# Softmax normalisation one step later in VectorE's queue: an MLA and stick-breaking trunk

## The chip, the cores and the metric

The kernel runs on one core of one Trainium2 chip. The metric is the device time of one execution in microseconds (us). Before the change it is 683.92 us, the median of three runs (682.63 to 685.81 us). The engines are named as the profile names them: PE (TensorE's matmuls), PEld (TensorE's weight loads), DVE (VectorE), ACT (ScalarE), POOL (GpSimd) and SP (the queue that issues the DMAs).

## The reference

The input is 512 positions of width 1024 in float32. A first layer is multi-head latent attention (MLA, 16 heads), a second one is stick-breaking attention that reads a shared K/V; each has a SiLU gate, an output projection and a gated per-layer embedding. The change touches the softmax of the first layer alone:

```
logits = jnp.einsum('bhqd,bhkd->bhqk', qi, k, preferred_element_type=jnp.float32) * scale
mask = s_idx[None, :] <= t_idx[:, None]
w = jax.nn.softmax(jnp.where(mask, logits, -jnp.inf), axis=-1)
return jnp.einsum('bhqk,bhkd->bhqd', w.astype(v.dtype), v)
```

Queries go in blocks of 128, so block j sees (j + 1) x 128 keys.

## The kernel before, in words

Every float32 product is made of three matmuls of high and low parts (`mm3`, L132 to L136). The MLA stage is a software pipeline of 64 steps, 16 heads by 4 query blocks (`layer`, L810). One step of the front (`mla_front`, L598) is:

- three score matmuls on PE into a PSUM tile of tag `s`, of which there are two (L604);
- the masking pass on DVE (L609; the lists of order below call it ISA): scores times the query's scale plus the mask into `e`, and the row's minimum into `sm`;
- Exp on ACT in place, with the row sum into another column of `sm` (L611);
- the reciprocal of that sum on DVE (L612);
- the product of `e` with it, on POOL (L614) or, for blocks 0 and 1 of the first eight heads, on DVE (L617).

Four steps later `pt_evac` (L555) transposes the normalised `e` on PE (L565, recorded at L130), and ACT and DVE split the result into high and low parts `pt` (L570, L571). After the fourth block of a head, `av` (L573) multiplies by V; ACT and DVE add its two halves (L591, L592: the head sum). `prep` of the next heads transposes q and k (`head_t`, L540) and splits them into `qk` (L548, L549, L551, L552). Between the steps stand matmuls of other work (the `windows` of L899: projections of the next four heads, gates, first halves of the output projection). Their PSUM tiles have tag `g`, two of them in this stage; what frees one is its evacuation, for a half projection the residual addition at L781, for a gate the product at L440, followed by a Sigmoid on ACT (L447) and a product on POOL (L448).

The tile framework orders each engine's instructions by a simulated timeline and by priorities: front, transposes and AV products have an offset of 50 (L46). Between the masking pass and the reciprocal of one step nothing but the data dependency decides.

Of the kernel before, what the change touches and what calls it, by code (L numbers as in the profile page):

```python
# [16 lines left out]
P = 128  # L17
S = 512
# [60 lines left out]
class Trunk:  # L79
    def __init__(self, ctx, tc, A):  # L80
        self.tc, self.nc, self.A = tc, tc.nc, A
        self.cp = ctx.enter_context(tc.tile_pool(name="cp", bufs=1))
        self.sp = ctx.enter_context(tc.tile_pool(name="sp", bufs=1))
        self.pp = ctx.enter_context(tc.tile_pool(name="pp", bufs=1, space=PSUM))
        self.dp = ctx.enter_context(tc.tile_pool(name="dp", bufs=1, space=DRAM))
        self.n = 0
        self.lin = False
        self.last_pe = None
        self.later = None

    BUFS = {"A": 8, "B": 10, "qk": 8, "hat": 6, "gate": 8, "v": 2, "f": 6, "e": 8, "ws": 3, "wh": 3, "wl": 3, "R": 1,
            "sm": 16, "smg": 3, "g": 2, "s": 2, "t": 4}
# [505 lines left out]
    def mla_front(self, h, j, qh, ql, kh, kl, sm, V):  # L598
        nc, v = self.nc, self.nc.vector
        n = (j + 1) * P  # L600
        nn = max(n, 2 * P)
        js = slice(j * P, n)
        ps = self.ps([P, S], "s")
        self.mm3(ps[:, 0:nn], qh[:, js], ql[:, js], kh[:, 0:nn], kl[:, 0:nn], True, True)  # L604
        e = self.t([P, S], F32, "e")
        st = self.t([P, 4], F32, "sm")
        i = j * GH + h % GH

        v.tensor_tensor_reduce(out=e[:, 0:n], in0=ps[:, 0:n], in1=self.mask[:, S - n:S], scale=sm[:, 1, i:i + 1],  # L609
                               scalar=3.0e38, op0=ALU.add, op1=ALU.min, accum_out=st[:, 0:1])  # L610
        nc.scalar.activation(e[:, 0:n], e[:, 0:n], AF.Exp, bias=st[:, 0:1], scale=-1.0, accum_out=st[:, 2:3])  # L611
        v.reciprocal(out=st[:, 3:4], in_=st[:, 2:3])  # L612
        if j >= (2 if h < NH // 2 else 0):
            nc.gpsimd.tensor_scalar(out=e[:, 0:n], in0=e[:, 0:n], scalar1=st[:, 3:4], scalar2=1.0,  # L614
                                    op0=ALU.mult, op1=ALU.mult)
        else:
            v.tensor_scalar(out=e[:, 0:n], in0=e[:, 0:n], scalar1=st[:, 3:4], scalar2=None, op0=ALU.mult)  # L617
        return e

    def sb_group(self, g, res):  # L620
        nc, A, v = self.nc, self.A, self.nc.vector
# [188 lines left out]
    def layer(self, windows, prep, front, pair, prep_lead, lead, av_lag, off):  # L810
        hp = self.tc.high_priority
        heads, es = {}, {}
        NS = NH * NT
        GS = GH * NT
        done = [0] * NG
        for i in range(-prep_lead, NS + lead + av_lag):
            ip = i + prep_lead
            if ip < NS:
                g = ip // GS
                if ip % NT == 0:  # L820
                    with hp(offset=off[0]):
                        heads[ip // NT] = prep(ip // NT, *self.groups[g])
                n, gen = windows[g]
                while done[g] * GS < n * (ip % GS + 1):
                    next(gen, None)
                    done[g] += 1
                if ip % GS == GS - 1:
                    for _ in gen:
                        pass
            if 0 <= i < NS:  # L830
                with hp(offset=off[1]):
                    es[i] = front(i // NT, i % NT, *heads[i // NT])
            b = i - lead
            if 0 <= b < NS:
                h, j = divmod(b, NT)
                if j > 0:
                    with hp(offset=off[2]):
                        self.pt_evac(h, j - 1, es.pop(b), es.pop(b - 1) if j == 1 else None)
            c = b - av_lag
            if 0 <= c < NS and c % NT == NT - 1:  # L840
                h = c // NT
                with hp(offset=off[3]):
                    self.av(h, heads[h][-1])
                if h % 2:
                    pair(h // 2)
# [203 lines left out]
```

## Time and profile before

| | |
|---|---|
| median of three runs | 683.92 us |
| the profiled execution | 683.51 us, span 681.7 us |
| busy: PE, PEld, DVE, ACT, POOL | 666.2, 560.9, 476.7, 400.7, 356.8 us |
| chain that ended last, by engine | PE 89%, ACT 4%, DVE 4%, POOL 1% |
| MLA stage | about 85 to 262 us of the span |

Matmuls are pipelined and their ends are modelled: one of 512 columns is listed with about 0.4 us but the next starts 0.227 us after it. An engine's idle time is listed before the instruction that ended it, with the instruction that released it. Engines take their own instructions in order, so a waiting instruction holds those behind it.

### The profile page before, as it was taken

The page shows a single profiled execution, that of the slowest core. Times are in us where ns is not written, and L with a number is a line of the kernel's source. Part 1 is how long each engine was busy: PE and PEld are TensorE (multiplying, and loading weights), DVE is VectorE, ACT ScalarE, POOL GpSimd, SP SyncE. Part 2 cuts the span into 40 slices and gives each one's busy share as a digit, 9 for nine tenths or more (in the row PEclk, how much of TensorE's full clock was granted, in tenths as well). Part 3 has the DMA queues.
Part 4 walks back from the last instruction along what each step waited for, and adds up shares of the span by engine and source line. Part 5 has one row for each costly group of instructions (what it writes and reads, how often), then busy time and mean ns, then how long its engine had stood idle before and what let it go on. Part 6 is the DMA issues. An engine that isn't in the chain of part 4 may idle for free.

```text
span 681.7 us, 10052 instructions
## 1 busy us (share of the span) xinstructions
PE 666.2 (98%) x3598; PEld 560.9 (82%) x3598; DVE 476.7 (70%) x868; ACT 400.7 (59%) x812; POOL 356.8 (52%) x293
## 2 busy tenths in 40 slices
PE   8989999999998999999999999999999999999997
PEld 6778898989877888888789788779879877788886
DVE  6866489987986774846853886876886889654332
ACT  7266496987988664444533666566665777432221
POOL 5737678776795550035443663775856677100130
PEclk9989999999999999999989999999999999999999
DMA  7331302100133110734332222111221222442321
GB/s 242 116 120 56 109 32 66 62 17 17 35 110 105 62 62 32 210 118 136 119 128 62 94 87 67 59 68 34 91 67 59 64 93 84 162 125 93 107 80 62
DMA packets 21762, 59.82 MB, mean 88 GB/s; under 512 B 2896, under 2 KB 3664, under 8 KB 21712
## 3 DMA queue, kind: packets, MB, share of 16 engines
q1 hardware_dynamic: 21712, 59.18, 26.9%
q8 instruction: 28, 0.46, 0.3%
q14 instruction: 22, 0.18, 0.1%
HBM read 54.97 MB, written 4.19 MB: 87 GB/s over the span
## 4 chain that ended last, share of the span: by engine, by line
PE 89%; ACT 4%; DVE 4%; issue 1%; POOL 1%; DMA 0%; ACTq 0%; POOLq 0%
PE g L127 41%; PE t L127 25%; PE s L127 16%; PE t L130 6%; DVE A L161 1%; ACT L447 1%; ACT wh L143 1%; DVE e L609 1%; DVE ptl L571 0%; DMA e<-in_xT 0%; POOL f L326 0%; DVE f L804 0%; ACT L611 0%; ACT f L447 0%; ACT e L611 0%
## 5 line engine op out<-in xcount | busy, mean ns | idle before, releaser
L127 PE MATMUL g<-A,wh 128*128 128x512 f32 x560 | 182.6, 405 | 2.1 <-ACT f L802 1.4
L143 ACT CAST wh<-ws 128x1024 fp32r<-128x1024 f32 (+2 forms) x92 | 90.2, 982 | 106.3 <-issue 41.0
L144 DVE TENSOR_TENSOR wl<-ws,wh 128x1024 fp32r<-128x1024 f32 (+2 forms) x72 | 96.8, 1346 | 47.0 <-ACT wh L143 45.9
L127 PEld LDWEIGHTS g<-A,wh 128*128 128x128 f32 x560 | 99.6, 189 | 25.4 <-issue 3.2
L127 PE MATMUL g<-A,wl 128*128 128x512 f32 x280 | 110.9, 396 | 0.7 <-POOL wl L344 0.7
L182 POOL TENSOR_TENSOR ws<-ws,gc 128x1024 f32<-128x1024 f32 x24 | 52.2, 2177 | 62.7 <-DMA ws<-in_w_sq 25.2
L698 POOL TENSOR_TENSOR e<-e,e 128x384 f32<-128x384 f32 (+1 forms) x48 | 61.9, 1309 | 20.0 <-DVE e L697 17.1
L570 ACT CAST pth<-t 128x384 fp32r<-128x384 f32 (+1 forms) x96 | 49.6, 518 | 32.0 <-PE t L130 31.3
L571 DVE TENSOR_TENSOR ptl<-t,pth 128x384 fp32r<-128x384 f32 (+1 forms) x96 | 56.5, 593 | 14.8 <-ACT pth L570 14.3
L127 PEld LDWEIGHTS g<-A,wl 128*128 128x128 f32 x280 | 52.9, 189 | 13.2 <-POOL wl L344 1.6
L127 PE MATMUL t<-A,wh 128*128 128x512 f32 (+1 forms) x192 | 59.1, 393 | 0.0
L130 PE MATMUL t<-ident,e 128*128 128x128 f32 x320 | 55.4, 272 | 0.0
L697 DVE TENSOR_TENSOR_SCAN e<-e,maskb 128x384 f32<-128x384 f32 (+1 forms) x32 | 45.8, 1471 | 8.2 <-ACT e L686 8.2
L130 PEld LDWEIGHTS t<-ident,e 128*128 128x128 f32 x320 | 40.4, 140 | 7.3 <-POOL e L614 0.2
L144 POOL TENSOR_TENSOR wl<-ws,wh 128x1024 fp32r<-128x1024 f32 (+2 forms) x20 | 40.0, 2002 | 12.2 <-ACT wh L143 10.7
L127 PE MATMUL s<-qk,qk 96*128 96x256 f32 (+1 forms) x192 | 44.4, 338 | 1.4 <-ACT qk L548 0.7
L614 POOL TENSOR_SCALAR e<-e,sm 128x384 f32<-128x384 f32 (+3 forms) x48 | 27.6, 579 | 33.3 <-DVE sm L612 28.7
L611 ACT ACTIVATE e<-e,sm 128x128 f32<-128x128 f32 (+1 forms) x64 | 36.3, 568 | 12.6 <-DVE sm L609 10.8
L127 PE MATMUL g<-wh,B 128*128 128x384 f32 (+1 forms) x136 | 43.4, 376 | 0.3 <-DVE v L538 0.3
L127 PE MATMUL g<-wh,A 128*128 128x256 f32 x208 | 42.4, 289 | 0.0
L127 PEld LDWEIGHTS t<-A,wh 128*128 128x128 f32 (+1 forms) x192 | 35.1, 184 | 8.3
L127 PE MATMUL t<-ptl,v 128*128 128x256 f32 (+2 forms) x128 | 39.5, 329 | 1.8 <-DVE ptl L571 1.8
(291 smaller groups left out, 1607.2 us busy)
## 6 DMA issues: line engine op xcount, KB each, us to landing
ws<-in_w_pg SPq DMA_DIRECT2D x16, 512.0 KB, 3.6
ws<-in_w_g SPq DMA_DIRECT2D x8, 512.0 KB, 3.2
ws<-in_w_o SPq DMA_DIRECT2D x16, 256.0 KB, 2.6
ws<-in_w_k SPq DMA_DIRECT2D x8, 512.0 KB, 3.6
ws<-in_w_sq SPq DMA_DIRECT2D x8, 512.0 KB, 3.5
ws<-in_w_v SPq DMA_DIRECT2D x8, 512.0 KB, 3.6
ws<-in_w_sg SPq DMA_DIRECT2D x8, 512.0 KB, 3.5
ws<-in_w_o SPq DMA_DIRECT2D x8, 512.0 KB, 3.6
```

The lines of the kernel that those rows point to most:

```text
L127: return self.pe(self.nc.tensor.matmul(*a, **kw))
L130: return self.pe(self.nc.tensor.transpose(*a))
L143: nc.scalar.copy(out=wh, in_=src)
L144: lo_engine.tensor_tensor(out=wl, in0=src, in1=f32(wh), op=ALU.subtract)
L161: (lo_engine or nc.vector).tensor_tensor(out=lo, in0=src, in1=f32(hi), op=ALU.subtract)
L182: nc.gpsimd.tensor_tensor(out=ws, in0=ws, in1=gain.unsqueeze(2).to_broadcast((P, nk, P)), op=ALU.mult)
L570: nc.scalar.copy(out=views[0], in_=ps)
L571: nc.vector.tensor_tensor(out=views[1], in0=ps, in1=f32(views[0]), op=ALU.subtract)
L611: nc.scalar.activation(e[:, 0:n], e[:, 0:n], AF.Exp, bias=st[:, 0:1], scale=-1.0, accum_out=st[:, 2:3])
L614: nc.gpsimd.tensor_scalar(out=e[:, 0:n], in0=e[:, 0:n], scalar1=st[:, 3:4], scalar2=1.0, op0=ALU.mult, op1=ALU.mult)
L697: v.tensor_tensor_scan(out=x, data0=x, data1=mask[:, ::-1], initial=0.0, op0=ALU.mult, op1=ALU.max)
L698: nc.gpsimd.tensor_tensor(out=b[:, 0:n], in0=b[:, 0:n], in1=om[:, 1:n + 1], op=ALU.mult)
```

## The change

The reciprocal and the product of a step are put off to the next step's front. There, right after the masking pass of the new step has been issued, the old step's reciprocal is issued with an ordering edge behind that pass on DVE; then its product. The last step's pair is issued without an edge, one turn later. The arithmetic and the number of instructions in the source stay the same.

```diff
-        v.tensor_tensor_reduce(out=e[:, 0:n], in0=ps[:, 0:n], in1=self.mask[:, S - n:S], scale=sm[:, 1, i:i + 1],
+        low = v.tensor_tensor_reduce(out=e[:, 0:n], in0=ps[:, 0:n], in1=self.mask[:, S - n:S], scale=sm[:, 1, i:i + 1],
                                scalar=3.0e38, op0=ALU.add, op1=ALU.min, accum_out=st[:, 0:1])
         nc.scalar.activation(e[:, 0:n], e[:, 0:n], AF.Exp, bias=st[:, 0:1], scale=-1.0, accum_out=st[:, 2:3])
-        v.reciprocal(out=st[:, 3:4], in_=st[:, 2:3])
+        self.norm_step(low)
+        self.unnormed = lambda: self.mla_norm(h, j, e, st)
+        return e
+
+    def norm_step(self, behind=None):
+
+        if self.unnormed is not None:
+            r = self.unnormed()
+            if behind is not None:
+                self.tc.add_manual_dep(r.ins, behind.ins.name,
+                                       mybir.DependencyInfo(mybir.DependencyClass.NoSync, mybir.DependencyReason.DATA),
+                                       reason="order")
+        self.unnormed = None
+
+    def mla_norm(self, h, j, e, st):
+        nc, v = self.nc, self.nc.vector
+        n = (j + 1) * P
+        r = v.reciprocal(out=st[:, 3:4], in_=st[:, 2:3])
         if j >= (2 if h < NH // 2 else 0):
...
-        return e
+        return r
...
             if 0 <= i < NS:
                 with hp(offset=off[1]):
                     es[i] = front(i // NT, i % NT, *heads[i // NT])
+            if i == NS:
+                self.norm_step()
```

Lines move by 1 up to the masking pass (L609 becomes L610, L611 becomes L612), the reciprocal becomes L630, POOL's product L632, and L781 becomes L799. Since the framework orders all engines anew, rows move on PE, DVE, ACT and POOL through the whole MLA stage; SP's list stays as it was. In the rows below a tile's number tells it apart; with the change the same tile mostly has a number lower by 2.

**First place: ACT around steps 44 to 46, where gates' Sigmoids stand among Exps.** The rows L447 (then L448) are Sigmoids, L611 (then L612) Exps; the 128x128 and 128x256 Exps are steps 44 and 45. Before:

```order
## ACT: 750 rows
L447 ACT_TABLE_LOAD
L447 ACTIVATE f_2287<-gate_1771 128x512
L548 CAST qk_2327<-t_2322 96x512
L570 CAST pth_110<-t_2387 128x384
L143 CAST wh_2366<-ws_2364 128x512
L447 ACTIVATE f_2290<-gate_2192 128x512
L570 CAST pth_110<-t_2425 128x3x128
L160 CAST A_1339<-f_1214 128x512
L160 CAST A_1629<-f_1482 128x512
L570 CAST pth_110<-t_2441 128x4x128
L551 ACTIVATE qk_2453<-t_2448,hs 96x512
```

With the change, from the second Exp load of the piece on:

```order
## ACT: 752 rows
L612 ACT_TABLE_LOAD
L612 ACTIVATE e_2497,sm_2498<-e_2497,sm_2498 128x128
L161 CAST A_1337<-f_1212 128x512
L612 ACTIVATE e_2516,sm_2517<-e_2516,sm_2517 128x256
L161 CAST A_1627<-f_1480 128x512
L448 ACT_TABLE_LOAD
L448 ACTIVATE f_2288<-gate_2190 128x512
L161 CAST A_1903<-f_1763 128x512
L161 CAST A_2246<-f_2086 128x512
L612 ACT_TABLE_LOAD
L612 ACTIVATE e_2563,sm_2564<-e_2563,sm_2564 128x384
```

Before, the Sigmoids of gates 5 and 6 (gate_1771, gate_2192) stood under one load; now that of gate 6 (gate_2190) has moved down between the Exps of steps 45 and 46, with a load of its own and another one for the Exp behind it.

**Second place: DVE at steps 46 and 47, around the residual addition L781 (then L799), whose tile is gate_2362 (then gate_2360).** Before:

```order
L440 TENSOR_TENSOR gate_2282<-g_2210,R_678 128x512
L609 ISA e_2565,sm_2566<-s_2561,mask,smg_1281 128x384
L609 ISA sm_2566 128x1
L609 ISA e_2598,sm_2599<-s_2594,mask,smg_1281 128x512
L609 ISA sm_2599 128x1
L592 TENSOR_TENSOR f_2402<-t_2393,f_2402 64x512
L612 RECIPROCAL sm_2566<-sm_2566 128x1
L612 RECIPROCAL sm_2599<-sm_2599 128x1
L781 TENSOR_TENSOR gate_2362<-g_2337,f_2360 128x512
```

With the change:

```order
L610 ISA e_2596,sm_2597<-s_2592,mask,smg_1279 128x512
L610 ISA sm_2597 128x1
L630 RECIPROCAL sm_2564<-sm_2564 128x1
L441 TENSOR_TENSOR gate_2280<-g_2208,R_678 128x512
L550 TENSOR_TENSOR qk_2461<-t_2455,qk_2460 96x512
L593 TENSOR_TENSOR f_2400<-t_2391,f_2400 64x512
L572 TENSOR_TENSOR ptl_108<-t_2522,pth_106 128x384
L593 TENSOR_TENSOR f_2400<-t_2528,f_2400 64x512
L799 TENSOR_TENSOR gate_2360<-g_2335,f_2358 128x512
L162 TENSOR_TENSOR A_2540<-f_2400,A_2540 128x512
L610 ISA e_2644,sm_2645<-s_2640,mask,smg_1830 128x128
L630 RECIPROCAL sm_2597<-sm_2597 128x1
```

The reciprocal of step 47 (sm_2597) has moved behind the masking pass of step 48 and so behind the residual addition; the gate product, a qk split, a pt split and a head sum now stand ahead of that addition.

**Third place: PE ahead of the first score matmuls of step 44 (tile s_2495, then s_2493).** Before:

```order
L127 MATMUL t_2393<-ptl_108,v_1493 128x256
L127 MATMUL g_2210<-A_126,wh_2206 128x512 x2
L130 MATMUL t_2425<-ident,e_2264 128x128 x3
L127 MATMUL g_2210<-A_126,wl_2207 128x512
L127 MATMUL g_2210<-A_158,wh_2206 128x512
L127 MATMUL s_2495<-qk_2327,qk_2318 128x256
L127 MATMUL s_2514<-qk_2327,qk_2318 128x256
```

With the change:

```order
L128 MATMUL t_2391<-ptl_108,v_1491 128x256
L131 MATMUL t_2423<-ident,e_2262 128x128 x2
L131 MATMUL t_2439<-ident,e_2298 128x128 x2
L131 MATMUL t_2423<-ident,e_2262 128x128
L131 MATMUL t_2439<-ident,e_2298 128x128 x2
L128 MATMUL s_2493<-qk_2325,qk_2316 128x256
L128 MATMUL s_2512<-qk_2325,qk_2316 128x256
L128 MATMUL g_2114<-A_331,wh_2110 128x512 x2
```

Four matmuls of the second gate (g_2210) and the last three of the first (two of them the last row here, the third some rows further) have moved behind these scores, and four transposes of step 39 (t_2439) ahead of them.

## Rows read from the trace of the kernel before

**Rows 1.** The page, busy time, share of the span and instructions:

```profile
PE 666.2 (98%) x3598; PEld 560.9 (82%) x3598; DVE 476.7 (70%) x868; ACT 400.7 (59%) x812; POOL 356.8 (52%) x293
```

**Rows 2.** Stretches: length, busy time (instructions) by engine, clock, DMA share, GB/s:

```profile
core 0: us, PE busy (x) PEld busy (x) DVE busy (x) ACT busy (x) POOL busy (x), PEclk, DMA share, GB/s
...
185.00:210.00 25.00, 22.22 (x116) 17.88 (x115) 18.14 (x39) 22.57 (x38) 22.78 (x20) 1.00 0.32 96
210.00:240.00 30.00, 30.00 (x180) 26.35 (x179) 22.39 (x57) 20.23 (x49) 13.85 (x17) 1.00 0.27 89
...
sum 187.00, PE 183.19 PEld 159.88 DVE 146.03 ACT 145.74 POOL 124.58; mean PE 20.35 PEld 17.76 DVE 16.23 ACT 16.19 POOL 13.84
```

**Rows 3.** Waits of PE, 75 to 262 us: total us, times, longest:

```profile
PE g L127 <- DVE gate L781: 2.1, 1, 2.1
PE s L127 <- ACT qk L548: 0.7, 1, 0.7
PE s L127 <- ACT v L537: 0.4, 1, 0.4
PE s L127 <- DVE sm L609: 0.4, 2, 0.2
PE g L127 <- DVE v L538: 0.3, 1, 0.3
```

**Rows 4.** Waits of all engines, 75 to 262 us:

```profile
POOL e L614 <- DVE sm L612: 28.7, 17, 3.5
...
DVE sm L612 <- ACT e L611: 10.2, 15, 1.4
...
PEld t L130 <- POOL e L614: 0.2, 1, 0.2
```

**Rows 5.** DVE in order of time: start, length, instruction, idle before:

```profile
208.06 0.16 DVE L612 RECIPROCAL sm<-sm 128x1 f32<-128x1 f32 x1 [1.34 <-ACT e L611]
208.76 0.17 DVE L612 RECIPROCAL sm<-sm 128x1 f32<-128x1 f32 x1 [0.54 <-ACT e L611]
208.84 0.69 DVE L781 TENSOR_TENSOR gate<-g,f 128x512 f32<-128x512 f32 x1
```

**Rows 6.** PE in order of time:

```profile
193.00 0.51 PE L127 MATMUL s<-qk,qk 96*128 96x256 f32 x2 [0.69 <-ACT qk L548]
...
209.59 0.73 PE L127 MATMUL g<-B,wh 128*128 128x512 f32 x2 [2.09 <-DVE gate L781]
```

**Rows 7.** Groups by shape, 75 to 262 us: busy us, mean ns, idle before:

```profile
L612 DVE RECIPROCAL sm<-sm 128x1 f32<-128x1 f32 x64 | 9.8, 155 | 10.4 <-ACT e L611 10.2
...
L611 ACT ACT_TABLE_LOAD x4 | 5.1, 1283 | 0.1
...
L447 ACT ACT_TABLE_LOAD x3 | 3.8, 1283 | 0.7 <-DVE gate L440 0.7
```

**Rows 8.** DVE in order of time, steps 26 and 27:

```profile
147.52 0.16 DVE L612 RECIPROCAL sm<-sm 128x1 f32<-128x1 f32 x1 [0.38 <-ACT e L611]
147.81 0.75 DVE L609 CUSTOM_DVE_ANT_0 e<-s,mask,smg 128x512 f32<-128x512 f32 x1
```

**Rows 9.** POOL in order of time, products of steps 26 and 27:

```profile
152.25 1.31 POOL L614 TENSOR_SCALAR e<-e,sm 128x384 f32<-128x384 f32 x2
```

**Rows 10.** PE in order of time, transposes of step 26:

```profile
158.79 0.49 PE L130 MATMUL t<-ident,e 128*128 128x128 f32 x3
```

**Rows 11.** The chain in order of time, merged: start, length, instructions:

```profile
140.74 1.31 PE t L130 x12
...
295.70 5.44 PE g L127 x24
```

**Rows 12.** ACT in order of time, around a table load and a later split:

```profile
187.73 0.68 ACT L551 ACTIVATE qk<-t,hs 96x512 fp32r<-96x512 f32 x1
188.42 1.28 ACT L611 ACT_TABLE_LOAD   x1
189.72 0.73 ACT L611 ACTIVATE e<-e,sm 128x512 f32<-128x512 f32 x1
...
192.85 0.47 ACT L570 CAST pth<-t 128x384 fp32r<-128x384 f32 x1
```

More of the change, by code (lines that the diff above doesn't have):

```diff
@@ L607, in mla_front @@
         i = j * GH + h % GH
-        v.tensor_tensor_reduce(out=e[:, 0:n], in0=ps[:, 0:n], in1=self.mask[:, S - n:S], scale=sm[:, 1, i:i + 1],
+        low = v.tensor_tensor_reduce(out=e[:, 0:n], in0=ps[:, 0:n], in1=self.mask[:, S - n:S], scale=sm[:, 1, i:i + 1],
                                scalar=3.0e38, op0=ALU.add, op1=ALU.min, accum_out=st[:, 0:1])
         nc.scalar.activation(e[:, 0:n], e[:, 0:n], AF.Exp, bias=st[:, 0:1], scale=-1.0, accum_out=st[:, 2:3])
-        v.reciprocal(out=st[:, 3:4], in_=st[:, 2:3])
+        self.norm_step(low)
[8 more added lines that the diff above has]
+                                       reason="order")
+        self.unnormed = None
+    def mla_norm(self, h, j, e, st):
+        nc, v = self.nc, self.nc.vector
+        n = (j + 1) * P
+        r = v.reciprocal(out=st[:, 3:4], in_=st[:, 2:3])
         if j >= (2 if h < NH // 2 else 0):
```

## The prediction

> **What bounds the kernel now.** I read the busy shares first, then the stretches, then the waits, then single rows. TensorE (PE) is busy for 98% of the span [rows 1]. The softmax stage runs from 85 to 262 us; of the 187 us from 75 on, PE is busy 183.19 us at full granted clock, so it is idle for 3.81 us, and 2.78 us of that lies between 185 and 210 us; from 210 to 240 us it is never idle [rows 2]. The reader is to see there that no edit of VectorE's (DVE's) queue can give back more than about 3.8 us unless it also changes PE's own work, which this one doesn't. The waits say what those gaps are: 2.1 us once for the residual addition at L781, 0.7 us once for ScalarE's (ACT's) copy of the next head's keys at L548, and smaller ones of at most 0.4 us [rows 3]. What the change is aimed at is large but elsewhere: DVE's reciprocal waits 10.2 us in all for ACT's Exp, and GpSimd (POOL) 28.7 us for the reciprocal [rows 4]. Both engines have room, so these sums are no price; they count only where PE stands behind them.
>
> **That place** is 207 to 209.6 us. Two reciprocals wait for two Exps, at 208.06 and 208.76 us; the addition L781 stands behind them and starts at 208.84 us [rows 5], and the matmul that needs the PSUM buffer freed by it starts at 209.59 us after 2.09 us of idle [rows 6]. Behind the two Exps stands ACT: Sigmoid (gates) and Exp alternate here, and each change of function is a table load of 1283 ns, seven in the window [rows 7].
>
> **The change, part by part.** *The reciprocal itself.* 64 instructions of 155 ns [rows 7] stay on DVE, none added: 0 in work. Each is now behind the next step's L609. *The product.* It follows the reciprocal, so it comes later. For steps 26 and 27: step 26's reciprocal ran at 147.52 us, step 27's L609 started at 147.81 us and takes 0.75 us [rows 8]; so the reciprocal moves to about 148.6 us, 1.0 us later. POOL made the products of steps 26 and 27 from 152.25 to 153.56 us [rows 9], and the transposes of step 26 that read them start at 158.79 us [rows 10]. The first product ends near 152.9 us, which leaves 5.9 us of cover for a delay of 1.0 us. I cost the lateness at 0; if a step had no cover, its transposes would stand still for the 1.0 us. Nothing is moved on the DMA queue: SP's list is the same, so loads cost 0.
>
> *The wait in front of L781.* With the change one reciprocal is already behind an L609, and the other comes after L781 (second place of the order rows). But L781 now also stands behind a gate product that moved down, a qk split, a pt split and a second head sum, which ACT feeds. Bounds: the whole 2.09 us goes, or none of it. PE also reaches that point with more work done first: three matmuls of 512 columns at 0.227 us, four score matmuls of 256 columns at about half that, and nine transposes at 0.109 us [rows 11], 2.1 us together. Following ACT's new list row by row with the durations of the old rows, I get a wait of about 1.1 us: **-1.0 us**.
>
> *The order on ACT.* The reordering has a side effect: gate product 6 falls behind two mask passes on DVE, its Sigmoid falls between Exps, and two more table loads appear (first place of the order rows; ACT's list is 750 rows, then 752). A load is 1.28 us, and the rows around one show nothing else: the copy ahead ends at 188.41 us, the load starts at 188.42 us, the Exp at 189.72 us [rows 12]. Two loads are 2.6 us of ACT in a stretch where ACT is busy 22.57 of 25 us [rows 2]. So its slack there is 2.4 us, and the cost lies between 0 (all in the slack) and 2.6 us (all on the path).
> The Trainium skill, "ScalarE: Activation LUTs", What ACT_TABLE_LOAD costs, puts a change of set at the same 1283 ns and adds about 1380 ns of drain, 2.66 us in all; by it the two loads would be 5.3 us. The gaps of 0.01 and 0.02 us beside this load show no such drain, so the trace agrees with the load and not with the drain.
>
> Of the 2.6 us I place two pieces. *First piece, at the scores of step 44* (third place of the order rows): PE now comes to these scores with 7 fewer 512-column matmuls and 4 more transposes behind it, 7 x 0.227 - 4 x 0.109 = 1.15 us sooner [rows 11]. It used to arrive at 192.31 us and to wait 0.69 us, until 193.00 us [rows 6]. The copy it waits for stands behind the same ACT rows as before plus one pt copy of 0.47 us [rows 12]. Ready at 193.5 us, arrival at 191.2 us: a wait of 2.3 us in place of 0.69, **+1.6 us**. *Second piece:* a load now stands before the Exp of step 48, where none stood; the pt copy behind it frees the PSUM buffer for the next head sum. PE had no idle time there [rows 2]. Bounds 0 and 2.6 us; my walk down the list gives up to 1.9 us, of which I take half, since ACT waited for POOL and DVE between these rows: **+1.0 us**.
>
> *Elsewhere.* The other 1.0 us of PE's idle time (3.81 - 2.78) is five short waits on data that arrives as before; it may go or be replaced: 0, with -1.0 and +1.0 for the range. The second layer and the output part are unchanged.
>
> Sum: -1.0 + 1.6 + 1.0 = +1.6 us. The profiled execution took 683.51 us (span 681.7 us and 1.8 us around it), 0.41 us under the median 683.92 us of three. That gives 685.1 us on the first and 685.5 us on the second; I say **685.3 us**, 0.2% up, which a measurement of this kernel cannot tell from none: it tells about 0.5%, 3.4 us.
>
> **The rivals.** *Faster: the blocked DVE queue was the whole cause.* Then the waits at 193 and 209.6 us go (2.78 us), and perhaps all the 3.81 us: 680.7 us or at best 679.7 us on the profiled time. For it: L781 did wait for reciprocals that waited for Exp. Against it: the two loads more, and the fact that a gain above 3.4 us needs nearly all idle time of the stage to vanish. A gain over 0.5%: 0.08. A small gain inside 0.5%: 0.25.
>
> *Slower: ACT becomes the bound between 185 and 225 us.* Here both loads land on the path in full (2.6 us), the wait at L781 stays because its ACT inputs are later, and the first piece comes on top: 1.6 + 2.6 = +4.2 us, 687.7 us. It decides from the point at which ACT's slack of 2.4 us is used up, so that every later row of ACT is PE's wait: then the sum passes 3.4 us. For it: ACT was busy 90% there, and POOL's products stand behind long GpSimd rows in the same stretch. Against it: from 210 us on PE had no idle time at all, so other work was ready. Chance of more than 0.5%: 0.15.
> A drain of 1.38 us at each of the two switches, the Trainium skill's figure in the section named above, would send it there too (683.51 + 5.3 = 688.8 us); the rows showed none.
>
> *Slower: the products come too late.* If the cover of 5.9 us at steps 26 and 27 is not typical, PE stops at the transposes, 1.0 us for every step missed; four such steps make 4 us, 687.5 us. For it: the lead is four steps, and one goes. Against it: PE's weight load waited for POOL's product once, 0.2 us [rows 4]. 0.07.
>
> *The change does nothing:* the order of DVE's rows could have stayed. The lists show it moved, so what remains is that it moves only hidden time; that is the forecast's neighbour, within 0.5%.
>
> **How the numbers follow.** Forecast, 0 to +3.4 us: 0.45. Small gain: 0.25. Together within 0.5%: 0.70. Faster by more: 0.08. Slower by more: 0.15 + 0.07 = 0.22. The range takes the lower end at 681.5 us (most of the two big waits gone and nothing new) and the upper at 688.8 us (4.2 us of ACT and a missed step over the profiled time); outside are some 0.1 on either side.
>
> **What would show it.** In the profile after: nine table loads of ACT in the stage, not seven; DVE's reciprocals no longer waiting 10.2 us for Exp; PE's wait for L548 up from 0.7 to about 2.3 us; its wait for L781 down to about 1 us; new waits near 215 us, on pt or head-sum buffers. I am wrong in the sum if the wait at the scores of step 44 is not longer, wrong in the mechanism if PE's idle time in the stage changes outside 185 to 225 us by over 1 us, or if transposes wait for POOL's products.

## The result, and the profile after

The changed kernel takes 691.11 us (median of 7 runs, 687.53 to 692.12) against 683.92 us for the one before: a ratio of 1.0099, 95% interval 1.0079 to 1.0119. It is slower by 5.4 to 8.1 us. The forecast was 685.3 us with a range of 681.5 to 688.8 us, and "within 0.5%" as the likeliest case; the result lies outside both.

The profiled run took 691.11 us with a span of 689.3 us. The page's busy times, as [rows 1]:

```profile
PE 669.5 (97%) x3598; PEld 563.6 (82%) x3598; DVE 486.6 (71%) x868; ACT 402.5 (58%) x814; POOL 352.9 (51%) x293
```

DVE has the same 868 instructions as before but 9.9 us more busy time. ACT has two instructions more, the two table loads that were forecast (nine in the stage, where seven stood). The stretches of the kernel after, columns as in [rows 2]:

```profile
75.00:262.00 187.00, 178.50 (x1027) 155.93 (x1026) 150.23 (x382) 144.58 (x354) 121.52 (x120) 0.99 0.18 56
120.00:140.00 20.00, 17.35 (x100) 15.51 (x98) 17.64 (x46) 15.19 (x44) 14.31 (x16) 0.91 0.17 53
140.00:180.00 40.00, 38.51 (x237) 35.09 (x238) 36.93 (x94) 30.45 (x85) 23.21 (x21) 1.00 0.05 14
185.00:210.00 25.00, 22.62 (x120) 18.49 (x120) 19.25 (x41) 23.62 (x46) 18.75 (x19) 1.00 0.20 64
210.00:240.00 30.00, 28.20 (x162) 23.45 (x160) 21.19 (x54) 24.47 (x53) 16.11 (x18) 1.00 0.27 89
340.00:360.00 20.00, 18.24 (x77) 14.52 (x76) 12.45 (x15) 7.89 (x15) 9.01 (x5) 0.83 0.42 132
```

and three of them of the kernel before:

```profile
120.00:140.00 20.00, 19.32 (x122) 17.55 (x121) 18.98 (x55) 18.64 (x53) 15.25 (x17) 1.00 0.15 53
140.00:180.00 40.00, 39.83 (x246) 36.08 (x245) 32.81 (x105) 32.43 (x91) 29.90 (x30) 1.00 0.08 27
340.00:360.00 20.00, 19.92 (x94) 16.25 (x93) 11.69 (x13) 7.86 (x12) 9.19 (x5) 0.91 0.37 112
```

Two things are to be read here. PE's idle time from 75 to 262 us went from 3.81 us [rows 2] to 8.50 us (187 - 178.50), and most of the new part lies from 120 to 180 us: 0.85 us before (0.68 + 0.17), 4.14 us now (2.65 + 1.49). And the granted clock, 1.00 in these stretches before, is 0.91 from 120 to 140 us: part of it ran at 1.2 GHz. From 340 to 360 us, where every engine has the rows of before in the order of before, some 7 us later, it fell from 0.91 to 0.83. (PE's lower busy time there is mostly no new wait: the 1.50 us for which PE stands ahead of 342.3 us are 1.43 us ahead of 335.6 us in the kernel before, outside that stretch.)

So two sums are needed. For every run I take the span times its mean granted clock, which is the time that the span would have at full clock, and the rest, which was lost to half clock (the clock is given to three digits, so each is good to 0.4 us). The first is an estimate: it counts the time in which PE stands as if it went with the clock. Over 22 runs of the kernel before that is 675.7 us and 6.5 us; over the 7 runs of the kernel after 680.2 us and 8.5 us. **Of the loss about 4.5 us is time that PE stood, and about 2.0 us is clock.** By the spread of the runs the first is known to 0.7 us either way and the second to 1.6 us (95%); the first agrees with the 4.7 us by which PE's idle time in the stage rose.

The waits of PE from 75 to 262 us, as [rows 3]:

```profile
PE s L128 <- DVE sm L610: 2.2, 3, 1.5
PE t L128 <- DVE ptl L572: 1.6, 2, 0.8
PE t L131 <- DVE hat L531: 1.3, 1, 1.3
PE t L131 <- DVE f L593: 1.0, 1, 1.0
PE s L128 <- ACT qk L549: 0.7, 1, 0.7
...
PE g L128 <- DVE gate L799: 0.4, 1, 0.4
```

and two of the waits of all engines, as [rows 4]:

```profile
POOL e L632 <- DVE sm L630: 30.4, 20, 3.4
...
DVE sm L630 <- ACT e L612: 2.7, 4, 1.4
```

The aim was reached: the reciprocal waits 2.7 us for Exp in place of 10.2 us, and the residual addition costs PE 0.4 us in place of 2.1 us. But PE now waits longer for DVE elsewhere: for masking passes, pt splits, a rotary product and a head sum. DVE itself, by groups of equal shape, after:

```profile
L494 DVE TENSOR_SCALAR smg<-smg 128x16 f32<-128x16 f32 x3 | 5.2, 1719 | 0.2 <-POOL smg L493 0.2
L635 DVE TENSOR_SCALAR e<-e,sm 128x256 f32<-128x256 f32 x8 | 5.5, 686 | 0.0
```

and before:

```profile
L493 DVE TENSOR_SCALAR smg<-smg 128x16 f32<-128x16 f32 x3 | 2.5, 824 | 0.0
L617 DVE TENSOR_SCALAR e<-e,sm 128x256 f32<-128x256 f32 x8 | 3.2, 402 | 0.1
```

The same instructions on the same shapes got slower: the sign change of 16 query scales from 0.82 to 1.72 us, the 128x256 softmax product from 0.40 to 0.69 us. Two rows show what happens, one of these sign changes and a rotary product. DVE in order of time, after:

```profile
130.07 2.69 DVE L494 TENSOR_SCALAR smg<-smg 128x16 f32<-128x16 f32 x1
132.68 0.74 DVE L610 CUSTOM_DVE_ANT_0 e<-s,mask,smg 128x512 f32<-128x512 f32 x1
...
158.55 2.58 DVE L531 TENSOR_TENSOR hat<-krot,smg 128x256 f32<-128x256 f32 x1
```

POOL:

```profile
130.09 2.65 POOL L145 TENSOR_TENSOR wl<-ws,wh 128x1152 fp32r<-128x1152 f32 x1
...
158.06 2.80 POOL L145 TENSOR_TENSOR wl<-ws,wh 128x1024 fp32r<-128x1024 f32 x1
```

and PE:

```profile
133.48 0.62 PE L128 MATMUL s<-qk,qk 96*128 96x256 f32 x3 [1.51 <-DVE sm L610]
134.63 0.61 PE L128 MATMUL s<-qk,qk 96*128 96x384 f32 x2 [0.54 <-DVE sm L610]
...
161.28 0.61 PE L131 MATMUL t<-ident,hat 128*96 128x128 f32 x4 [1.35 <-DVE hat L531]
```

A DVE row of 16 columns takes 2.69 us, about as long as POOL's split of 128x1152 beside it (2.65 us), and both end within 0.02 us of each other; step 19's masking pass stands behind it, and PE behind the masking pass. The rotary product at 158.55 us ends only after POOL's split of 128x1024 and holds PE for 1.35 us. I call such a row **held**. Counted against the lower quartile of the rows of the same line and shape, 8 rows of DVE took over 0.6 us too long between 75 and 275 us before, 9.0 us together; after it is 11 rows and 15.2 us.

### The profile page after: what moved, and what is told of

Same layout as the page of the kernel before. It is cut to its first block, busy times and chain, and to the rows that moved or that the text cites. A ratio compares the mean times of both kernels' runs of the same rounds, so it can differ in the third digit from the quotient of the medians.

```text
span 689.3 us, 10064 instructions
## 1 busy us (share of the span) xinstructions
PE 669.5 (97%) x3598; PEld 563.6 (82%) x3598; DVE 486.6 (71%) x868; ACT 402.5 (58%) x814; POOL 352.9 (51%) x293
## 4 chain that ended last, share of the span: by engine, by line
PE 73%; DVE 9%; ACT 6%; POOL 5%; issue 3%; DMA 3%; SPq 0%; POOLq 0%; DVEq 0%; ACTq 0%
PE g L128 33%; PE t L128 22%; PE s L128 14%; PE t L131 5%; DVE e L715 2%; DVE wl L145 1%; DMA ws<-in_w_c 1%; DMA ws<-in_pT 1%; POOL smg L493 1%; ACT e L612 1%; DVE ptl L572 1%; POOL f L327 1%; POOL e L716 1%; POOL wl L145 1%; ACT L612 1%
## 5 line engine op out<-in xcount | busy, mean ns | idle before, releaser
L145 DVE TENSOR_TENSOR wl<-ws,wh 128x1024 fp32r<-128x1024 f32 (+2 forms) x72 | 98.8, 1373 | 47.9 <-ACT wh L144 47.4
L612 ACT ACTIVATE e<-e,sm 128x128 f32<-128x128 f32 (+1 forms) x64 | 36.5, 572 | 24.6 <-DVE sm L610 15.0
L632 POOL TENSOR_SCALAR e<-e,sm 128x384 f32<-128x384 f32 (+3 forms) x48 | 28.7, 604 | 34.3 <-DVE sm L630 30.4
L128 PE MATMUL t<-pth,v 128*128 128x256 f32 (+2 forms) x128 | 40.9, 329 | 1.6 <-DVE ptl L572 1.6
```

The source lines that it names most:

```text
L128: return self.pe(self.nc.tensor.matmul(*a, **kw))
L145: lo_engine.tensor_tensor(out=wl, in0=src, in1=f32(wh), op=ALU.subtract)
```

## The experiments

**How rows were kept in place.** The framework orders all engines anew for any edit. To change one thing alone, each kernel below fixes the whole order of either kernel, engine by engine and row by row, with ordering edges like those of the change, and moves only the rows named:

```diff
-        Trunk(ctx, tc, A).run()
+        Trunk(ctx, tc, A).run(), pin(tc)
...
+    for e, ks in order.items():
+        for a, b in zip(ks, ks[1:]):
+            tc.add_manual_dep(made[e][b], made[e][a].name,
+                              mybir.DependencyInfo(mybir.DependencyClass.NoSync, mybir.DependencyReason.DATA),
+                              reason="order")
```

"Before" in the table is what the same chip gave for the kernel before in the same session; the last two columns are means over the runs, as above (the kernel before: 675.1 to 675.8 us and 6.3 to 6.7 us). By the spread of the runs a difference from the kernel before is known to some 0.7 to 1.5 us (95%) in the column at full clock and to 0.7 to 1.9 us in the last one. No run fixes an order without moving a row; the nearest to one are 683.22 us in the old order (step 13 with POOL's split later) and 691.30 us in the new one (four loads fewer), both within 0.7 us of the kernels whose order they keep, so no cost of the fixing itself shows.

| kernel | median | before | ratio, 95% interval | at full clock | lost to half clock |
|---|---|---|---|---|---|
| changed kernel | 691.11 | 683.92 | 1.0079 to 1.0119 | 680.2 | 8.5 |
| 34 late reciprocals, old order | 687.20 | 683.95 | 1.0024 to 1.0081 | 679.4 | 6.3 |
| early reciprocals, new order | 692.36 | 683.95 | 1.0098 to 1.0149 | 681.2 | 9.4 |
| new order, sign change later | 686.19 | 683.95 | 1.0025 to 1.0052 | 680.2 | 4.4 |
| new order, four loads fewer | 691.30 | 683.95 | 1.0056 to 1.0114 | 680.5 | 7.8 |
| new order, three rows moved | 687.05 | 683.51 | 1.0031 to 1.0068 | 677.7 | 7.8 |
| sign change later, four loads fewer | 690.40 | 683.51 | 1.0081 to 1.0116 | 680.0 | 8.8 |
| late in heads 0 to 7 alone | 687.12 | 683.51 | 1.0030 to 1.0069 | 679.5 | 5.9 |
| late in heads 8 to 15 alone | 683.80 | 683.51 | 0.9973 to 1.0010 | 677.0 | 4.5 |
| steps 13 and 21 alone | 687.82 | 683.59 | 1.0038 to 1.0084 | 678.7 | 7.6 |
| heads 0 to 7 without 13 and 21 | 683.78 | 683.59 | 0.9990 to 1.0025 | 676.7 | 5.6 |
| step 13 alone | 684.44 | 683.88 | 0.9996 to 1.0033 | 678.0 | 4.8 |
| step 13, POOL's split later | 683.22 | 683.88 | 0.9979 to 1.0003 | 675.1 | 6.2 |
| step 21 alone | 684.44 | 683.88 | 0.9986 to 1.0031 | 676.5 | 6.3 |
| old order, two loads more | 684.85 | 683.88 | 1.0000 to 1.0028 | 677.6 | 5.4 |
| old order, L781 first | 679.42 | 683.59 | 0.9923 to 0.9965 | 673.4 | 4.5 |
| L781 first, late in heads 8 to 15 | 682.29 | 683.59 | 0.9967 to 1.0010 | 675.5 | 5.5 |

**1. The edit without the new order.** Of the 63 reciprocals with a next step, 35 stood ahead of its masking pass before; 34 are moved behind it, as here for step 13:

```diff
-L612 RECIPROCAL sm_1316<-sm_1316 128x1
 L440 TENSOR_TENSOR gate_1220<-g_1106,R_678 128x512
 L617 TENSOR_SCALAR e_1293<-e_1293,sm_1294 128x128
-L617 TENSOR_SCALAR e_1315<-e_1315,sm_1316 128x256
 L609 ISA e_1357,sm_1358<-s_1353,mask,smg_505 128x384
 L609 ISA sm_1358 128x1
+L612 RECIPROCAL sm_1316<-sm_1316 128x1
+L617 TENSOR_SCALAR e_1315<-e_1315,sm_1316 128x256
```

> The edit without the new order: every engine keeps the order of the kernel before, row by row, and on DVE alone 34 of the 35 reciprocals that stood ahead of the next step's masking pass are moved right behind it (with the 7 DVE products that hang on them); step 47 stays, since other rows need it there. Theory of the order (the loss comes from the order that was made anew on all engines, not from the place of the reciprocals): no loss, 682 to 684 us, PE idle time between 75 and 262 us at most 3.8 us, the wait for L781 of 2.1 us shorter or gone. Theory of the edit (late reciprocals cost): 687 us or more, with PE waits on transposes for POOL's products. Theory of the table loads: unchanged, since there are seven loads as before.

Measured 687.20 us, +3.3 us. Neither theory had it: the late reciprocals do cost in the old order, though no transpose waits for POOL's products by more than 0.5 us.

**2. The new order without the edit.** The reciprocals of the same 35 steps, put back, for example:

```diff
+L630 RECIPROCAL sm_1002<-sm_1002 128x1
 L610 ISA e_1043,sm_1044<-s_1039,mask,smg_505 128x128
 L610 ISA sm_1044 128x1
-L630 RECIPROCAL sm_1002<-sm_1002 128x1
```

> The new order without the edit: every engine keeps the order of the changed kernel, row by row, and on DVE alone the reciprocals of the 35 steps that stood ahead of the next masking pass before are put back, each right ahead of that pass. Theory of the order: still slow, 688 to 692 us, with the held DVE row at about 130 us and PE idle of 6 us or more between 75 and 262 us. Theory of the edit: back to 684 to 686 us. Theory of the table loads: still nine loads, so 686 us or more.

Measured 692.36 us: no better than the changed kernel. Within the new order the place of the reciprocals is worth nothing that shows (1.0 us more at full clock, known to 1.0 us); the order is slow by itself.

**3. One row of the new order.**

```diff
-L494 TENSOR_SCALAR smg_1279<-smg_1279 128x16
 L610 ISA e_1530,sm_1531<-s_1526,mask,smg_850 128x512
...
 L630 RECIPROCAL sm_1664<-sm_1664 128x1
+L494 TENSOR_SCALAR smg_1279<-smg_1279 128x16
```

> The changed kernel's order with one row moved: the sign change of 16 query scales on DVE (L494, 128x16, held for 2.69 us at 130 us while POOL runs its split of 128x1152) is put 15 rows later, behind the masking passes of five more steps, to a place where POOL was idle. Theory of the held row: the two PE gaps at 132 to 134.6 us (1.51 + 0.53 us) go, and if the lower clock at 136 to 139 us came from them, 1.7 us more: 2 to 4 us faster than the changed kernel, 687 to 689 us. Theory of the edit or of the table loads: no change, 690 to 691 us.

Measured 686.19 us, 12 runs from 685.40 to 687.69 us, better than the 687 to 689 us of the theory: a single row of 16 columns, moved, takes 4.9 us off the changed kernel. DVE in that run:

```profile
131.46 2.08 DVE L635 TENSOR_SCALAR e<-e,sm 128x256 f32<-128x256 f32 x1
...
137.57 0.15 DVE L494 TENSOR_SCALAR smg<-smg 128x16 f32<-128x16 f32 x1
```

The sign change takes 0.15 us at its new place, but the softmax product that now stands beside POOL's split is held 2.08 us instead. That is why the time at full clock stays at 680.2 us: the gap moved (0.96 us at 133 us, 1.44 us at 137 us). What the row bought is clock: 4.4 us were lost to half clock, not 8.5, and in the profiled run none of it in the MLA stage. The verdict of the theory was right and its first reason only in part.

**4. Three rows of the new order.** To the edit above:

```diff
-L635 TENSOR_SCALAR e_1459<-e_1459,sm_1460 128x256
 L630 RECIPROCAL sm_1511<-sm_1511 128x1
...
 L610 ISA sm_1604 128x1
+L635 TENSOR_SCALAR e_1459<-e_1459,sm_1460 128x256
...
-L635 TENSOR_SCALAR e_1854<-e_1854,sm_1855 128x128
 L529 TENSOR_TENSOR hat_1489<-hat_1489,smg_1279 128x8x64
 L531 TENSOR_TENSOR hat_1489<-krot,smg_1279 128x8x32
 L553 SCALAR_TENSOR_TENSOR qk_1810<-t_1804,hs,qk_1809 96x512
+L635 TENSOR_SCALAR e_1854<-e_1854,sm_1855 128x128
```

> The changed kernel's order with three DVE rows moved: the sign change of before (L494), and two products of the softmax step on DVE (L635) that were held by POOL's split in the run of that kernel: the 128x256 one (2.08 us at 131.5 us) goes behind the masking passes of two more steps, the 128x128 one at 155 us goes behind the two query products L529 and L531, so that L531 comes before POOL's split. Theory of the held rows: the PE gaps of 0.96, 1.44 and 1.34 us at 133, 137 and 158 us shrink by 2 to 3.5 us in all, to 683 to 684.5 us, as the kernel before. Theory that the reciprocals' lateness costs by itself: 685.5 us or more. Theory of the table loads: no change, 686 us, since nine loads stay.

Measured 687.05 us, a miss by the time. At full clock it is the 2.5 us that were expected (680.2 to 677.7 us), and the wait for L531 is gone from the list; but 7.8 us were lost to half clock in place of 4.4, and the gain with them.

**5. Four table loads fewer in the new order.** On ACT two Sigmoids go down, behind Exps (gate 6 shown here, gate 4 moves likewise); alone, and together with the edit of 3:

```diff
-L448 ACT_TABLE_LOAD
-L448 ACTIVATE f_2288<-gate_2190 128x512
 L161 CAST A_1903<-f_1763 128x512
 L161 CAST A_2246<-f_2086 128x512
-L612 ACT_TABLE_LOAD
 L612 ACTIVATE e_2563,sm_2564<-e_2563,sm_2564 128x384
 L144 CAST wh_2476<-ws_2474 128x1024
 L612 ACTIVATE e_2596,sm_2597<-e_2596,sm_2597 128x512
+L448 ACT_TABLE_LOAD
+L448 ACTIVATE f_2288<-gate_2190 128x512
```

> The changed kernel's order with two rows moved on ACT: the Sigmoid of gate 4 goes behind the Exp of step 43, and that of gate 6 behind the Exp of step 47, so that gates 4 and 5, and 6 and 7, share a table load; four loads fewer, 5.1 us of ACT between 193 and 220 us. Theory of the table loads: 1.5 to 4 us faster than the changed kernel, the PE gaps at 197.6, 214.8, 216.8 and 221 us (2.5 us together) shrink or go. Theory of the held rows: less than 1.5 us, the gaps before 190 us (5 us) and the lower clock at 136 us stay, 689 us or more.

> The sign change moved as before, and the two Sigmoids moved as before (four table loads fewer), together, so that the loads are priced where the race between the sign change and POOL's split no longer blurs it. Theory of the table loads: 1.5 to 4 us faster than the run with the sign change alone (686.2 us), 682 to 684.7 us. Theory that ACT's slack takes the loads: within 0.7 us of 686.2 us.

Measured 691.30 and 690.40 us: the first no better than the changed kernel, the second 4.2 us worse than the edit of 3 alone. The time at full clock is the same in all four (680.0 to 680.5 us). What the loads gave back was taken on POOL, here of the second kernel:

```profile
208.09 1.29 POOL L449 TENSOR_TENSOR gate<-gate,f 128x512 f32<-128x512 f32 x1 [4.14 <-ACT f L448]
```

POOL's product for gate 6 waits 4.14 us for the Sigmoid that was moved down; the softmax products, the split and the gating behind it come later, and at 217.32 us PE waits 2.09 us for a masking pass. As a test of the loads this is inconclusive.

The profiled run of the first kernel, its best of 9 with 684.62 us, shows the hold as a race. DVE:

```profile
129.61 0.15 DVE L494 TENSOR_SCALAR smg<-smg 128x16 f32<-128x16 f32 x1
129.68 0.74 DVE L610 CUSTOM_DVE_ANT_0 e<-s,mask,smg 128x512 f32<-128x512 f32 x1
...
130.34 2.10 DVE L635 TENSOR_SCALAR e<-e,sm 128x256 f32<-128x256 f32 x1
```

and POOL:

```profile
129.63 2.67 POOL L145 TENSOR_TENSOR wl<-ws,wh 128x1152 fp32r<-128x1152 f32 x1
```

DVE's order around here is that of the changed kernel, and both rows are listed 0.02 us apart in both; there the sign change was held 2.69 us, here it got through in 0.15 us. The masking pass runs beside the split at its usual 0.74 us. The product behind it is held until the split ends.

**6. The two halves of the edit, in the old order.** Heads 0 to 7 (16 reciprocals and 7 products on DVE) and heads 8 to 15 (18 reciprocals, all products on POOL), moved as in 1.

> The first half of the edit alone: the order of the kernel before on every engine, 16 reciprocals of the first eight heads (steps below 32) moved behind the next masking pass, with the 7 DVE products that hang on them. Theory of the held rows: the cost that the run with 34 reciprocals showed (3.2 us) lies here, since only here does a product run on DVE, behind the masking pass and ahead of head sums and splits: 686 to 688 us. Theory that every late reciprocal costs the same: half of it, 685.5 us.

> The second half of the edit alone: the order of the kernel before, 18 reciprocals of the last eight heads moved behind the next masking pass; POOL makes all their products. Theory of the held rows: no cost, and the wait for L781 (2.09 us at 207.5 us) shorter: 682 to 684 us. Theory that every late reciprocal costs the same: 685.5 us.

Measured 687.12 and 683.80 us. By the time, the whole cost is in the half where a product on DVE goes with the reciprocals. The other half is not free for all that: at full clock it costs 1.3 us (677.0 against 675.8, known to 0.8 us), which its clock gave back (4.5 us lost in place of 6.3), and on top of another kernel it cost 2.9 us (experiment 10).

**7. Two steps of the first half, and the other fourteen.** As in 1, for steps 13 and 21 alone, and for the rest.

> Only two steps of the edit, in the order of the kernel before: the reciprocals of steps 13 and 21, each with its 128x256 product on DVE, moved behind the next masking pass. In the run with 34 late reciprocals the first product was held 2.35 us by POOL's split at 120 us and the second stood at 140.8 us ahead of a head sum and the V scale that frees the matmuls' buffer. Theory that the DVE product in the wrong place is the cost: these two alone give nearly all of the 3.2 us, 686 to 687.5 us. Theory that the 16 late reciprocals of the first half share it: 684 to 684.5 us.

> The other 14 steps of the first half, without steps 13 and 21, in the order of the kernel before; five of them have a product on DVE. Theory that two products in the wrong place are the cost: as the kernel before, 683 to 684.5 us. Theory that the late reciprocals share it: 686 to 687 us.

Measured 687.82 us for the two and 683.78 us for the other fourteen. By the time, two steps of sixteen bring all of it. At full clock the two cost 3.6 us and the other fourteen 1.6 us (676.7 against 675.1, known to 0.8 us; in the profiled run PE is idle for 5.16 us from 75 to 262 us, where it was 3.81 us), and a clock that lost 1.1 us less hides most of that.

**8. Which of them, and by what.** Step 13 alone; step 21 alone; and step 13 with POOL's split out of its way:

```diff
+L614 TENSOR_SCALAR e_1357<-e_1357,sm_1358 128x384
 L144 TENSOR_TENSOR wl_1654<-ws_1651,wh_1653 128x1024
-L614 TENSOR_SCALAR e_1357<-e_1357,sm_1358 128x384
```

> The order of the kernel before with step 13 alone: its reciprocal and its 128x256 product on DVE behind the next masking pass. Theory of the held row: the product falls beside POOL's split of 128x1024, is held some 2.35 us, the masking pass of step 15 and PE come 1 to 1.5 us later: 684.5 to 685.5 us. Theory that step 21 is the cost: as before, 683.6 us.

> The order of the kernel before with step 21 alone: its reciprocal and its 128x256 product on DVE behind the next masking pass, ahead of a head sum and of the V scale. Theory that the row's place is the cost: PE gaps of 0.8 and 1.2 us in place of 0.37 and 0.31 us near 138 us, and a stretch of half clock (1.7 us) behind them in most runs: 685.5 to 687 us. Theory that POOL's hold is the only cost: as before, 683.6 us.

> As the run with step 13 alone, and on POOL the split of 128x1024 is put one row later, behind the 128x384 product of step 14, so that DVE's product no longer falls beside it. Theory of the held row: the product takes 0.35 us, not 2.35, at the same place in DVE's queue, PE's gap near 122 us (0.47 us) goes, 683 to 684 us. Theory that the later place costs by itself: as the run with step 13 alone.

Measured 684.44, 684.44 and 683.22 us. The times alone tell none of the three from the kernel before, and step 21 came out below the 685.5 us of its theory; what follows rests on the rows and on the column at full clock. DVE, POOL and PE with step 13 alone:

```profile
118.64 2.35 DVE L617 TENSOR_SCALAR e<-e,sm 128x256 f32<-128x256 f32 x1
```

```profile
118.45 2.39 POOL L144 TENSOR_TENSOR wl<-ws,wh 128x1024 fp32r<-128x1024 f32 x1
```

```profile
122.18 0.39 PE L127 MATMUL s<-qk,qk 96*128 96x256 f32 x1 [0.51 <-DVE sm L609]
```

DVE with the split moved, and POOL:

```profile
118.93 0.35 DVE L617 TENSOR_SCALAR e<-e,sm 128x256 f32<-128x256 f32 x1
```

```profile
121.21 2.40 POOL L144 TENSOR_TENSOR wl<-ws,wh 128x1024 fp32r<-128x1024 f32 x1
```

The same product at the same place in DVE's list takes 2.35 us beside the split and 0.35 us without it. At full clock step 13 costs 2.3 us (678.0 against 675.7) and nothing with the split moved (675.1). So the hold is the cost there, not the later place. The difference of these two kernels is 2.8 us, known to 0.9 us.

Step 21 costs 0.8 us at full clock, known to 0.7 us, and PE has two longer gaps with it. PE before, and PE and DVE with step 21 alone:

```profile
137.88 0.60 PE L127 MATMUL s<-qk,qk 96*128 96x256 f32 x3 [0.37 <-ACT v L537]
139.12 0.47 PE L127 MATMUL g<-wh,B 128*128 128x512 f32 x1 [0.31 <-DVE v L538]
```

```profile
138.04 0.60 PE L127 MATMUL s<-qk,qk 96*128 96x256 f32 x3 [0.51 <-DVE sm L612]
140.13 0.47 PE L127 MATMUL g<-wh,B 128*128 128x512 f32 x1 [1.17 <-DVE v L538]
```

```profile
138.01 0.74 DVE L617 TENSOR_SCALAR e<-e,sm 128x256 f32<-128x256 f32 x1
```

The V scale (L538) comes later because the product stands ahead of it; but the product takes 0.74 us and not 0.35 us, beside a POOL row of 0.73 us that starts at 137.87 us, so some of the cost is a hold here too. How much the place alone costs was not tried. The two steps add up to 3.1 us, and together they measured 3.6 us (678.7 against 675.1); the half clock makes up the rest of their 4.2 us.

**9. Two table loads more in the old order.**

```diff
-L447 ACTIVATE f_2290<-gate_2192 128x512
...
 L611 ACTIVATE e_2499,sm_2500<-e_2499,sm_2500 128x128
 L160 CAST A_1905<-f_1765 128x512
+L447 ACT_TABLE_LOAD
+L447 ACTIVATE f_2290<-gate_2192 128x512
+L611 ACT_TABLE_LOAD
 L611 ACTIVATE e_2518,sm_2519<-e_2518,sm_2519 128x256
```

> The order of the kernel before with one row moved on ACT: the Sigmoid of gate 6 stands between the Exps of steps 44 and 45, which adds two table loads (nine in place of seven, 2.57 us of ACT near 200 us) and nothing else. Theory of the table loads, on which the forecast rested: 1.0 to 2.6 us slower than before, 684.6 to 686.2 us, with a longer PE wait near 190 to 215 us. Theory that ACT's slack takes them: within 0.7 us of the kernel before, 683 to 684.3 us.

Measured 684.85 us, +1.0 us (interval 0 to 1.9 us), and 1.9 us at full clock. The waits of PE show both sides:

```profile
PE g L127 <- DVE A L161: 1.0, 1, 1.0
...
PE g L127 <- ACT A L160: 0.8, 1, 0.8
...
PE g L127 <- DVE gate L781: 0.5, 1, 0.5
```

Two new waits of 1.8 us stand behind the late Exp and the splits after it, and the wait for L781 falls by 1.6 us, since PE arrives there later. In this profiled run PE's idle time from 75 to 262 us is 4.17 us, only 0.36 us above that of before. The loads cost something, within the bounds that the prediction gave them, but an interval that begins at 0 does not say how much.

**10. What the change was for, in one row.** In the order before, the residual addition goes ahead of the two reciprocals that wait for Exp [rows 5]:

```diff
 L592 TENSOR_TENSOR f_2402<-t_2393,f_2402 64x512
+L781 TENSOR_TENSOR gate_2362<-g_2337,f_2360 128x512
 L612 RECIPROCAL sm_2566<-sm_2566 128x1
 L612 RECIPROCAL sm_2599<-sm_2599 128x1
-L781 TENSOR_TENSOR gate_2362<-g_2337,f_2360 128x512
```

> One row of the kernel before moved: the residual addition L781 at 208.84 us goes ahead of the two reciprocals that wait for Exp, and nothing else changes. Theory that this wait bounds PE there: the 2.09 us of PE idle time at 207.5 us shrink to 0.7 us or less, 682 to 683 us. Theory that the gain is taken back by the next wait or by the clock: 683.5 to 684.5 us.

Measured 679.42 us, ratio 0.9944 (0.9923 to 0.9965): faster than both kernels, by 2.4 to 5.3 us against the one before, and better than the 682 to 683 us of the theory. DVE and PE:

```profile
205.30 0.67 DVE L781 TENSOR_TENSOR gate<-g,f 128x512 f32<-128x512 f32 x1
206.71 0.16 DVE L612 RECIPROCAL sm<-sm 128x1 f32<-128x1 f32 x1 [0.74 <-ACT e L611]
```

```profile
206.03 0.73 PE L127 MATMUL g<-B,wh 128*128 128x512 f32 x2
```

The matmuls that waited 2.09 us [rows 6] start without a wait. At full clock the gain is 1.7 us (673.4 against 675.1 us, known to 0.9 us), near the 2.09 us of the wait; the other half is clock, 4.5 us lost in place of 6.7.

With the 18 late reciprocals of heads 8 to 15 on top:

> The candidate for a version that beats both kernels: the order of the kernel before, the 18 reciprocals of the last eight heads behind the next masking pass, and L781 ahead of the two reciprocals that wait for Exp. If the wait for L781 is what is left there: 681.5 to 682.5 us. If the new place of the 18 reciprocals only shifts waits: 683 to 684 us.

Measured 682.29 us, 2.9 us behind the single row. The late reciprocals do shift waits (PE stands 1.06, 0.57 and 0.68 us at 192.1, 203.3 and 209.4 us in that run); by what chain was not tried.

## Why the prediction was wrong, point by point

- **"Elsewhere: 0", with 1.0 us either way.** This is the step that failed. Outside 185 to 240 us I took the short waits for all that could change, on data "that arrives as before". It did not: in the new order DVE's rows fell beside POOL's long rows and were held, the masking pass at 132.68 us and the rotary product at 158.55 us came late, and from 120 to 180 us PE's idle time rose by 3.3 us; half clock followed at 136 us. With three such rows moved the new order loses 2.5 us less at full clock (experiment 4). The order lists showed that DVE's rows moved there too; I looked at what each row waits for, not at what runs beside it on POOL. The held rows stood in the trace of before, 8 of them, and no term of the sum priced one.
- **"I cost the lateness at 0."** Checked on POOL's products of steps 26 and 27. By the time it holds for POOL's products (experiment 6, second half: 683.80 us), though at full clock they cost 1.3 us; it is wrong for the steps whose product is on DVE, which I didn't look at: two of those cost 4.2 us.
- **The wait for L781: -1.0 us.** It went from 2.09 to 0.41 us: -1.7 us. Right in kind. Alone, the move gave 4.2 us, about half of it clock (experiment 10).
- **The scores of step 44: +1.6 us.** Not so: the wait for L549 is 0.73 us where it was 0.69 us for L548. PE came there at 197.63 us, 6.4 us later than I set it, and the copy was ready at 198.36 us, 4.9 us later: what I had worked out from the rows of before, PE's arrival above all, no longer held after the gaps ahead of it. Which of them did it was not tried.
- **The load before Exp of step 48: +1.0 us.** Nine loads came as forecast, and two loads more cost 1.0 us (0 to 1.9) when added by themselves. That is the size of the term, but those loads stood at steps 44 and 45; the one before step 48 was never priced by itself, and the run with four loads fewer did not settle it.
- **The region as a whole.** From 185 to 240 us idle time rose from 2.78 to 4.18 us (2.38 + 1.80), near the forecast +1.6 us. It is luck, and no success: 1.6 us of the 4.18 is one place at 188 to 190 us that no term named, where a head sum stands behind a held split.
- **The rivals.** "ACT becomes the bound" gave 687.7 us and "the products come too late" 687.5 us; neither is what happened. The second shows once: at 189.38 us a weight load waits 1.25 us for POOL's product, whose reciprocal stood behind that held split.
- **The clock** was in no term. The profile before showed 0.91 from 340 to 360 us, so it was there to be read.
- **The signs given.** The one for a wrong mechanism, idle time changed outside 185 to 225 us by over 1 us, is the one that came. The other one, transposes that wait for POOL's products, came once, with the 1.25 us.
- **Small slips**, which change nothing: the list of waits [rows 3] has four short ones and not five, and 683.5 + 4.2 + 1.0 us gives 688.7 us for the upper end, not 688.8.

What stays open: which rows of the new order make the last 2 us at full clock (677.7 us with three rows moved, 675.8 us before; the two table loads more, which cost 1.9 us at full clock in the old order, are a candidate that these runs leave standing), and what makes the clock fall in one run and not in the next.

## What to carry to other kernels

An ordering edge on one engine moves rows on all of them when a framework reorders; compare the orders where nothing was meant to change, and ask of every moved row what the other engines do at that moment. A DVE row on SBUF operands is best kept out of the shadow of a long POOL row, above all if a masking pass or a PSUM evacuation stands behind it. To free one late instruction, move that one: moving the row behind DVE's two waits gained 4.2 us, about half of it clock, and the rule for all 64 steps lost 7.2 us.

## What the hardware showed that was not expected

**Held rows.** DVE rows that read and write SBUF wait for a POOL row to end: 2.69 us for 0.15 us of work, 2.35 for 0.35 us, while the masking pass, which reads scores from PSUM and the mask from SBUF, ran beside the same split in its usual 0.74 us. Which of the two goes first is a race: rows listed 0.02 us apart went either way. The Trainium skill, "SBUF — State Buffer", Who interferes with whom, describes this: GpSimd's ports are VectorE's second pair, "Issue order, not op shape, decides who blocks", and the later one is blocked while the other's instruction runs. The runs agree on the block, with 2.35 us beside the split and 0.35 us without. On the order they show nothing: the trace lists DVE's row 0.02 us ahead of POOL's in both cases of the race.

**The clock.** A stretch at 1.2 GHz began 0.9 us after PE's gaps of 1.51 and 0.54 us at 132 to 134.6 us in the changed kernel, while gaps of 0.96 and 1.44 us at 133 to 138.6 us in the kernel of experiment 3 were followed by none. In the second layer the gap of 1.43 us at 334 us before and that of 1.50 us at 341 us after were both followed by such a stretch within 10 us, which cost 1.8 us in the one and 3.4 us in the other (20 us at 0.91 and at 0.83); a gap of 1.45 us at 339 us in the kernel of experiment 3 was followed by none (1.00 from 340 to 360 us). Runs of the same kernel differ: the mean granted clock of the changed kernel ranged from 0.984 to 0.993. In a comparison of less than 1% this is as large as what is looked for, so the time at full clock is worth a column of its own.
